# Attention on one Trainium2 core: blocks of probabilities kept whole and multiplied in fp32, or cut into two reduced-precision parts

## The chip, the cores and the metric

The kernel runs on one core of one Trainium2 chip. The metric is the time of one execution on the device in microseconds (us), as the median of several runs. An execution was also recorded by the hardware profiler, and all rows shown are from it. The engines are PE (TensorE matmul), PEld (its weight loads, which run beside the matmuls), DVE (VectorE), ACT (ScalarE), POOL (GpSimd) and SP (which issues most transfers).

## The reference

The program is two layers of a diffusion backbone over 1024 latent and 256 context tokens of width 1024, all in float32. The first layer mixes tokens by a chunked gMLP, the second by windowed attention; each is followed by a convolutional GLU. The change concerns the attention, in which 16 query heads share 4 key/value heads of 64 dimensions:

```
for each block of 128 queries j:
    kj, vj = k and v of blocks j-1, j, j+1
    s_lat  = (q @ kj^T) * 64^-0.5, masked to |q - k| <= 128
    s_ctx  = (q @ kc^T) * 64^-0.5                    # 256 context keys
    p      = softmax over [s_lat, s_ctx, sink]; the sink's column is dropped
    out[j] = p_lat @ vj + p_ctx @ vc
y = out @ w_o
```

So a query block sees five blocks of 128 keys: three of its window and two of the context. The first and the last query block have only two in the window, four in all.

## The kernel before

TensorE multiplies a full float32 operand in several passes. The kernel avoids that nearly everywhere: a float32 value is cut into two values of the type float32r, a high part (a cast, mostly on ACT) and a low part (value minus high part, on DVE), and a product of two such numbers is three single-pass matmuls (high by high, high by low, low by high).

In the attention the work is cut into 64 pairs of heads: 8 query blocks j, 4 key/value heads g, and two pairs `pr` for each. A loop over the pairs issues three steps, each for another pair, so that they overlap:

- `att_a` for pair i: the scores of two heads by TensorE (tiles `psA` and `psB` from `big`, the keys, and `tmp`, the queries), a masked running minimum of the negated scores on DVE (which leaves the scores in `tmp` for one head and in `wl` for the other, and the extremes in `sm`), the exponential on ACT, and the division on POOL.
- `att_b` for pair i - 2: each block of 128 keys of both heads is transposed by TensorE (`psB` from `ident` and `tmp` or `wl`), up to two blocks into one PSUM tile. The tile is then moved to SBUF in two parts: ACT casts it to the high part `PTh`, DVE subtracts that from the PSUM tile and writes the low part `PTl`. Both are tiles of the pool `act`, which has six buffers.
- `att_c` for pair i - 3: for each block the values `VV` (a tile called `y` in the profile, held as high part in 64 columns and low part in the other 64) are the weights, and `PTh` and `PTl` are multiplied one after the other, 256 columns each, into one PSUM tile `po`. The results by the high and the low part of the values stand in different partitions; ACT copies one half out (`tmp`) and DVE adds them into `row`.

Beside this the loop prepares queries (`q_prep`) and keys (`prep_k`, `build_k`), and, from pair 20 on, the output projection of finished rows of blocks (`o_steps`): attention rows go through DRAM (`oscr`) and come back as `oc`, to be multiplied with `wh` into `psA`. In pairs 8 to 23 the scores of the window and the context share one tile and one pass on DVE (`merged`).

The order on each engine is made by a scheduler from the order in which the loop issues the steps, its own estimates of durations, and the buffers. Each engine runs its instructions in that order and waits by semaphores. All instructions are issued through one helper, so all rows carry line 50, and it is the names of tiles that tell them apart.

Of the kernel before, what the change touches and what calls it, by code (L numbers as in the profile page):

```python
# [10 lines left out]
F32 = mybir.dt.float32  # L11
# [4 lines left out]
P = 128  # L16
# [16 lines left out]
def hybrid_kernel(  # L33
# [23 lines left out]
    V, S, G, T = Engine(nc.vector, "V"), Engine(nc.scalar, "S"), Engine(nc.gpsimd, "G"), Engine(nc.tensor, "T")  # L57
# [19 lines left out]
    def nm(s):  # L77
        uid[0] += 1
        return f"{s}_{uid[0]}"

    def t_raw():
        return sb.tile([P, 1024], F32, name=nm("raw"), tag="raw", bufs=3)
# [8 lines left out]
    def t_row(dt=F32, shape=(P, 1024)):  # L91
        return sb.tile(list(shape), dt, name=nm("row"), tag="row", bufs=10)
# [4 lines left out]
    def lead(tag):  # L97
        n = stage_pool["leads"].pop(tag, 0)
        if n:
            G.memset(stage_pool["pool"].tile([P, n], F32, name=nm("lead"), tag="lead" + tag, bufs=1), 0.0)  # L100

    def t_tmp(shape=(P, 640), dt=F32):
        return stage_pool["pool"].tile(list(shape), dt, name=nm("tmp"), tag="tmp", bufs=8)
# [5 lines left out]
    def t_act(shape=(P, 2, 640), dt=F32R):  # L109
        lead("act")  # L110
        return stage_pool["pool"].tile(list(shape), dt, name=nm("act"), tag="act", bufs=6)
# [21 lines left out]
    def psB(shape=(P, 512)):  # L133
        return ps.tile(list(shape), F32, name=nm("psB"), tag="psB", bufs=4)
# [1631 lines left out]
    qrows, qst, at = {}, {}, {}  # L1766
# [102 lines left out]
    def merged(j, g, pr):  # L1869
        return 8 <= 8 * j + 2 * g + pr < NM  # L1870
# [46 lines left out]
    run_post(20)  # L1917
    VV = hold["VV"]

    def att_b(j, g, pr):  # L1920
        nk = len(geo[j][1])
        Pt = at[(j, g, pr)]
        PTh, PTl = t_act((P, 5, 2, P)), t_act((P, 5, 2, P))
        for a in range(0, nk, 2):
            n = min(2, nk - a)
            pt = psB((P, 2, 2, P))
            for b in range(n):
                for h in range(2):
                    T.transpose(out=pt[:, b, h, :], in_=Pt[h][:, (a + b) * P:(a + b + 1) * P], identity=ident)
            S.copy(PTh[:, a:a + n], pt[:, 0:n])  # L1930
            V.tensor_sub(PTl[:, a:a + n], pt[:, 0:n], PTh[:, a:a + n])
        at[(j, g, pr)] = (PTh, PTl)

    orow, last_rows = {}, {}

    def att_c(j, g, pr):
        kts = geo[j][1]
        nk = len(kts)
        if merged(j, g, pr):
            kts = kts[-2:] + kts[:-2]  # L1940
        if j not in orow:
            orow[j] = t_row(shape=(P, KD, P))
        o = orow[j]
        PTh, PTl = at.pop((j, g, pr))
        po = psB((P, 2, P))
        for a in range(nk):
            lv = VV[:, kts[a], g, :]
            T.matmul(po, lv, PTh[:, a], start=(a == 0), stop=False)
            T.matmul(po, lv, PTl[:, a], start=False, stop=(a == nk - 1))
        ol = t_tmp((P, 2, P))  # L1950
        S.copy(ol[0:HD], po[HD:P])
        for h in range(2):
            V.tensor_tensor(out=o[h * HD:(h + 1) * HD, 2 * g + pr, :], in0=po[0:HD, h, :], in1=ol[0:HD, h, :],
                            op=ALU.add)
        if g == 3 and pr == 1:
            oh, ol_ = t_row(F32R, (P, KD, P)), t_row(F32R, (P, KD, P))
            S.copy(oh, o)
            V.tensor_sub(ol_, o, oh)
            if j >= 6:
                last_rows[j] = (oh, ol_)  # L1960
                return
            cs = slice(j * P, (j + 1) * P)
            S.dma_start(oscr[:, :, 0, cs], oh.bitcast(F32))
            Q.dma_start(oscr[:, :, 1, cs], ol_.bitcast(F32))
# [59 lines left out]
    for i in range(n_pairs + LC):  # L2024
        if i < n_pairs:
            j, g, pr = pairs[i]
            if j < 7 and pr == 1 and g in (1, 3):
                q_load(j + 1, g // 2)
            if pr == 1 and 1 < i < n_pairs - 1:
                q_prep(*pairs[i + 1][:2])  # L2030
            if i >= HEAD:
                att_a(j, g, pr)
            if j + 2 < 8:
                if g == 0 and pr == 1:
                    prep_k(j + 2)
                if g == 2 and pr == 0:
                    build_k(j + 2)
        if i in (21, 24, 27):
            t = 5 + (i - 21) // 3
            w = t_raw()[:, 0:512]  # L2040
            Q.dma_start(w, qraw[t - 5])
            qkv_post(t, 1, w)
        if i in (23, 26, 29):
            run_post()
        if LB <= i < n_pairs + LB:
            att_b(*pairs[i - LB])
        if LC <= i:
            att_c(*pairs[i - LC])
        while done < o_target(i):
            step(og)  # L2050
            done += 1
        tick()
# [68 lines left out]
```

## Time and profile before

| what | value |
|---|---|
| median of 3 runs | 2852.4 us (2848.68 to 2853.72) |
| the profiled execution | 2860.88 us, its span 2859.1 us |
| mean granted clock of TensorE | 0.988 of full |
| first score matmul of the loop to the last product with V | about 1797 to 2143 us |

The time of an execution is slightly longer than the span from the first to the last instruction. A busy share near 100% of PE does not say that TensorE is at its peak, because matmuls are pipelined and their rows overlap; the pace has to be read from the starts. Rows of groups give the busy time of all, the mean duration of one in ns, and the idle time before them with what ended it.

### The profile page before, as it was taken

The numbers are of one execution on the slowest core, as the hardware profiler recorded it, in microseconds if no ns is written. First come the engines' busy times: TensorE is split into PE (matmuls) and PEld (weight loads), VectorE is DVE, ScalarE is ACT, GpSimd is POOL, SyncE is SP. The second block draws the span as 40 slices with busy tenths as digits, with TensorE's granted clock in tenths as the row PEclk, the third lists the DMA queues.
The fourth block names the chain that finished last, engine by engine and source line by source line (L and its number), as shares of the span: only waits on it lengthen the run. The fifth ranks groups of instructions, "written<-read, shape, count | busy, mean of one in ns | idle before, by whom it ended". The sixth has DMA issues, their size and how long they took to land.

```text
span 2859.1 us, 40314 instructions
## 1 busy us (share of the span) xinstructions
PE 2741.8 (96%) x14570; PEld 2354.1 (82%) x14570; DVE 2221.8 (78%) x3466; ACT 1391.2 (49%) x2291; POOL 616.6 (22%) x806
## 2 busy tenths in 40 slices
PE   7999999999989999999999899999998999999998
PEld 5798887898889888888788778888887888888786
DVE  6567684787779899887776568898887788888776
ACT  4333242232367444455434545777876444445433
POOL 1164021360210212111000124543333121220000
PEclk9999999999999999999999999999999999999999
DMA  7775457554488355467855565347577345545753
GB/s 260 251 234 166 145 161 227 177 167 131 171 249 240 103 170 162 157 217 238 287 169 184 188 212 186 115 145 239 181 242 220 126 162 182 160 144 198 248 177 125
DMA packets 436335, 537.13 MB, mean 188 GB/s; under 512 B 20004, under 2 KB 300452, under 8 KB 436135
## 3 DMA queue, kind: packets, MB, share of 16 engines
q1 hardware_dynamic: 379575, 470.84, 51.4%
q10 hardware_dynamic: 55408, 59.52, 6.2%
q0 software_dynamic: 1152, 4.19, 0.4%
q8 instruction: 115, 1.88, 0.3%
q14 instruction: 85, 0.70, 0.1%
HBM read 414.40 MB, written 120.07 MB: 187 GB/s over the span
## 4 chain that ended last, share of the span: by engine, by line
PE 65%; DVE 13%; DMA 11%; ACT 5%; issue 4%; POOL 2%; SPq 1%; ACTq 0%; DVEq 0%; POOLq 0%
PE psB L50 48%; PE psA L50 16%; DVE row L50 3%; DVE wl L50 3%; DMA raw<-in_ada_w_dram 3%; DVE tmp L50 1%; DVE acc L50 1%; ACT wh L50 1%; ACT tmp L50 1%; DMA xT<-row 1%; DMA raw<-in_a_w_in_dram 1%; DVE y L50 1%; POOL sm L50 1%; DMA raw<-in_f_w_up_dram 1%; DMA raw<-in_f_w_down_dram 1%
## 5 line engine op out<-in xcount | busy, mean ns | idle before, releaser
L50 PE MATMUL psB<-cmb,wh 128*128 128x512 f32 (+2 forms) x2584 | 750.3, 374 | 7.2 <-ACT row L50 6.2
L50 PEld LDWEIGHTS psB<-cmb,wh 128*128 128x128 f32 x2584 | 471.9, 188 | 98.4 <-ACT row L50 8.1
L50 PE MATMUL psB<-cmb,wl 128*128 128x512 f32 (+2 forms) x1292 | 483.2, 374 | 0.2 <-DVE wl L50 0.2
L50 ACT CAST wh<-raw 128x1024 fp32r<-128x1024 f32 (+1 forms) x313 | 265.1, 863 | 441.6 <-PE psB L50 165.5
L50 DVE TENSOR_TENSOR wl<-raw,wh 128x1024 fp32r<-128x1024 f32 (+1 forms) x313 | 307.6, 997 | 106.6 <-ACT wh L50 104.9
L50 PEld LDWEIGHTS psB<-cmb,wl 128*128 128x128 f32 x1292 | 243.2, 188 | 44.0 <-DVE wl L50 0.8
L50 PE MATMUL psB<-wh,big 128*128 128x512 f32 x816 | 271.1, 398 | 3.7 <-ACT big L50 1.3
L50 ACT CAST wh<-row 128x1024 fp32r<-128x1024 f32 (+1 forms) x196 | 162.5, 834 | 186.8 <-DVE row L50 92.3
L50 PE MATMUL psB<-wh,act 128*128 128x512 f32 x640 | 200.1, 390 | 0.8 <-DVE tmp L50 0.8
L50 DVE TENSOR_TENSOR wl<-row,wh 128x1024 fp32r<-128x1024 f32 (+1 forms) x196 | 185.2, 948 | 12.2 <-ACT wh L50 11.8
L50 PE MATMUL psA<-big,wh 128*128 128x320 f32 x1024 | 193.2, 310 | 0.3 <-ACT row L50 0.3
L50 POOL TENSOR_TENSOR row<-raw,raw 128x512 f32<-128x512 f32 x44 | 68.5, 1558 | 574.2 <-DMA raw<-in_f_w_up_dram 490.8
L50 PEld LDWEIGHTS psB<-wh,big 128*128 128x128 f32 x816 | 154.3, 190 | 39.9 <-ACT tmp L50 2.4
L50 DVE SCALAR_TENSOR_TENSOR acc<-raw,ccols,acc 128x1024 f32<-128x1024 f32 x98 | 126.7, 1311 | 75.8 <-DMA raw<-in_ada_w_dram 75.5
L50 DVE SCALAR_TENSOR_TENSOR row<-row,cwcols,row 128x1024 f32<-128x1024 f32 (+2 forms) x142 | 152.6, 1075 | 39.2 <-ACT row L50 22.7
L50 ACT CAST ah<-raw 128x1024 fp32r<-128x1024 f32 x80 | 77.6, 974 | 201.6 <-PE psB L50 80.8
L50 DVE TENSOR_TENSOR row<-row,row 128x512 f32<-128x512 f32 (+4 forms) x169 | 155.9, 926 | 19.9 <-DMA row<-actd 12.2
L50 POOL TENSOR_SCALAR row<-row,sm,sm 128x128 f32<-128x128 f32 x160 | 144.1, 919 | 115.2 <-DMA row<-vscr 99.3
L50 PEld LDWEIGHTS psA<-big,wh 128*128 128x128 f32 x1024 | 159.9, 188 | 0.7 <-ACT row L50 0.5
L50 PE MATMUL psB<-wl,big 128*128 128x512 f32 x408 | 157.2, 395 | 0.9 <-DVE wl L50 0.9
L50 DVE TENSOR_TENSOR al<-raw,ah 128x1024 fp32r<-128x1024 f32 x80 | 90.2, 1128 | 71.9 <-ACT ah L50 71.6
L50 PE MATMUL psB<-row,wh 128*128 128x256 f32 x744 | 136.9, 286 | 8.2 <-ACT wh L50 6.7
(279 smaller groups left out, 6226.0 us busy)
## 6 DMA issues: line engine op xcount, KB each, us to landing
raw<-in_f_w_up_dram SPq DMA_DIRECT2D x121, 512.0 KB, 4.8
raw<-in_ada_w_dram SPq DMA_DIRECT2D x88, 512.0 KB, 4.4
raw<-in_a_w_in_dram SPq DMA_DIRECT2D x64, 512.0 KB, 4.8
wh<-woscr SPq DMA_DIRECT2D x48, 512.0 KB, 4.1
row<-actd SPq DMA_DIRECT2D x44, 512.0 KB, 5.5
actc<-row SPq DMA_DIRECT2D x44, 512.0 KB, 4.1
raw<-actc SPq DMA_DIRECT2D x40, 512.0 KB, 3.6
actd<-row SPq DMA_DIRECT2D x39, 512.0 KB, 2.7
```

Of the source, the lines that this page charges most:

```text
L50: ins = fn(*a, **kw)
```

## The change

In `att_b` some blocks stay whole: their transposed probabilities are copied once from PSUM to a float32 tile `PTw`, and no low part is made. For the first 20 pairs (the query blocks 0 and 1 and half of 2) these are blocks 0 to 3, later blocks 0, 1 and 4. The copy runs on ACT, except for blocks 2 and 3 of the first 20 pairs, where it runs on DVE. The remaining blocks are cut as before, and where there are at most two of them, high and low parts share one tile. In `att_c` a whole block is multiplied once, with the same values read as float32, in a full float32 product.

```diff
+    def whole(j, g, pr, a):
+        i = 8 * j + 2 * g + pr
+        return a < 4 if i < 20 else a in (0, 1, 4)
+
     def att_b(j, g, pr):
         nk = len(geo[j][1])
         Pt = at[(j, g, pr)]
-        PTh, PTl = t_act((P, 5, 2, P)), t_act((P, 5, 2, P))
+        wholes = [a for a in range(nk) if whole(j, g, pr, a)]
+        cut = [a for a in range(nk) if a not in wholes]
+        both = len(cut) > 2
+        PTw = t_act((P, 5, 2, P), F32) if wholes else None
+        PTh = t_act((P, 5, 2, P)) if cut else None
+        PTl = t_act((P, 5, 2, P)) if both else PTh
...
-            S.copy(PTh[:, a:a + n], pt[:, 0:n])
-            V.tensor_sub(PTl[:, a:a + n], pt[:, 0:n], PTh[:, a:a + n])
-        at[(j, g, pr)] = (PTh, PTl)
+            if a in wholes:
+                o = wholes.index(a)
+                (V.tensor_copy if a == 2 else S.copy)(PTw[:, o:o + n], pt[:, 0:n])
+                continue
+            o = cut.index(a)
+            ol = o if both else o + 2
+            S.copy(PTh[:, o:o + n], pt[:, 0:n])
+            V.tensor_sub(PTl[:, ol:ol + n], pt[:, 0:n], PTh[:, o:o + n])
+        at[(j, g, pr)] = parts
...
         for a in range(nk):
             lv = VV[:, kts[a], g, :]
-            T.matmul(po, lv, PTh[:, a], start=(a == 0), stop=False)
-            T.matmul(po, lv, PTl[:, a], start=False, stop=(a == nk - 1))
+            w = lv.bitcast(F32) if len(parts[a]) == 1 else lv
+            for n, x in enumerate(parts[a]):
+                T.matmul(po, w, x, start=(a == 0 and n == 0), stop=(a == nk - 1 and n == len(parts[a]) - 1))
```

The scheduler orders the stage anew. On PE, around the product with V of pair 28 (in the tile `psB_3056`; `act_3032` is its high part, `act_3033` its low part), there stands before:

```order
L50 MATMUL psB_3055_17986<-ident_69,tmp_3014_17789 128x128
L50 MATMUL psB_3055_17986<-ident_69,wl_3015_17790 128x128
L50 MATMUL psA_3007_17769<-wh_3039_17918,oc_3040_17920 128x512 x4
L50 MATMUL psB_3056_17991<-act_3032_17882,y_2391_14763 128x256
L50 MATMUL psB_3056_17991<-act_3033_17883,y_2391_14763 128x256
...
L50 MATMUL psA_3007_17769<-wh_3039_17918,oc_3040_17920 128x512 x2
L50 MATMUL psA_3064_18022<-big_2527_15607,tmp_3044_17943 128x384
```

High and low parts alternate, ten matmuls in all, with the projection's matmuls around them. On PE for the same pair (`act_3024` holds its three whole blocks, `act_3025` both parts of its two cut ones) there stands now:

```order
L50 MATMUL psB_3047_17815<-ident_69,tmp_3006_17629 128x128
L50 MATMUL psB_3047_17815<-ident_69,wl_3007_17630 128x128
L50 MATMUL psB_3048_17819<-act_3024_17717,y_2391_14763 128x256 x2
L50 MATMUL psB_3048_17819<-act_3025_17718,y_2391_14763 128x256 x4
L50 MATMUL psB_3048_17819<-act_3024_17717,y_2391_14763 128x256
L50 MATMUL psA_2999_17609<-wh_3031_17748,oc_3032_17750 128x512 x6
L50 MATMUL psA_3056_17847<-big_2527_15607,tmp_3036_17773 128x384
```

Seven instructions stand for ten, of which three are full float32 products, and the projection's six matmuls follow in one piece. On DVE, at `att_b` of pair 12 (low part `act_2760`; `ISA` is the masked minimum, with its extremes in `sm`), there stands before:

```order
L50 ISA wl_2756_16607,sm_2752_16603<-psA_2758_16616,mask_14494,nsnk_14504 128x640
L50 ISA sm_2752_16603 128x1
L50 TENSOR_TENSOR act_2760_16633<-psB_2761_16634,act_2759_16632 128x512
L50 TENSOR_TENSOR act_2760_16633<-psB_2762_16641,act_2759_16632 128x512
L50 TENSOR_TENSOR act_2760_16633<-psB_2763_16648,act_2759_16632 128x256
L50 ISA tmp_2772_16680,sm_2769_16677<-psA_2774_16682,mask_14494,nsnk_14504 128x640
```

On DVE for the same pair (whole blocks `act_2751`, the cut one `act_2752`) there stands now:

```order
L50 ISA wl_2748_16531,sm_2744_16527<-psA_2750_16540,mask_14494,nsnk_14504 128x640
L50 ISA sm_2744_16527 128x1
L50 COPY act_2751_16556<-psB_2754_16564 128x512
L50 TENSOR_TENSOR act_2752_16557<-psB_2755_16570,act_2752_16557 128x256
L50 TENSOR_TENSOR row_2710_16377<-psB_2756_16575,tmp_2757_16582 64x128 x2
L50 ISA tmp_2764_16598,sm_2761_16595<-psA_2766_16600,mask_14494,nsnk_14504 128x640
```

Two wide subtractions gave way to one copy between the same minima, and the final addition of an earlier pair moved up.

More of the change, by code (lines that the diff above doesn't have):

```diff
@@ L1922, in att_b @@
         Pt = at[(j, g, pr)]
-        PTh, PTl = t_act((P, 5, 2, P)), t_act((P, 5, 2, P))
+        wholes = [a for a in range(nk) if whole(j, g, pr, a)]
[4 more added lines that the diff above has]
+        PTl = t_act((P, 5, 2, P)) if both else PTh
+        parts = {}
+        for a in range(nk):
+            n = cut.index(a) if a in cut else wholes.index(a)
+            parts[a] = (PTw[:, n],) if a in wholes else (PTh[:, n], PTl[:, n if both else n + 2])
         for a in range(0, nk, 2):
@@ L1943, in att_c @@
         o = orow[j]
-        PTh, PTl = at.pop((j, g, pr))
+        parts = at.pop((j, g, pr))
         po = psB((P, 2, P))
```

## Prediction

> **What bounds the kernel now.** I read the totals of the page first, then the attention stage in windows, then who ends the waits of PE there, then its chain of waits, and last the timeline for the pace of single matmuls. All durations are of the profiled execution.
>
> ```profile
> span 2859.1 us, 40314 instructions
> PE 2741.8 (96%) x14570; PEld 2354.1 (82%) x14570; DVE 2221.8 (78%) x3466; ACT 1391.2 (49%) x2291; POOL 616.6 (22%) x806
> ```
>
> PE is the engine of this kernel. The change lies in the attention stage alone, from the first scores (1797 us) to the last product with V (2143 us). The windows row gives for a stretch: length, then busy time and instructions of PE, PEld, DVE, ACT and POOL, the granted clock, the DMA share and GB/s.
>
> ```profile
> 1797.00:1937.00 140.00, 130.17 (x959) 118.11 (x958) 126.27 (x372) 112.34 (x274) 72.17 (x119) 0.99 0.42 136
> 1937.00:2143.00 206.00, 195.05 (x1337) 175.07 (x1335) 175.00 (x601) 155.54 (x356) 66.81 (x96) 0.98 0.66 218
> 1797.00:2143.00 346.00, 325.22 (x2293) 293.18 (x2291) 301.27 (x973) 267.88 (x629) 138.98 (x214) 0.99 0.56 185
> ```
>
> I cut at 1937 because pair 25 is multiplied with V there. Up to it DVE is busy 90% and PE 93%; behind it PE is at 95% and DVE at 85%. The chain of waits of the two stretches says the same in another way:
>
> ```profile
> by line: PE psB L50 27.9%; PE psA L50 16.6%; DVE tmp L50 8.7%; DVE act L50 7.4%; issue 7.2%; ACT act L50 5.2%; ACT tmp L50 4.9%; DVE row L50 4.9%; DMA qraw<-act 4.7%; ACT wl L50 4.1%; DVE wl L50 4.1%; ACT big L50 1.0%; DVE raw L50 0.9%; DVE
> ...
> by line: PE psB L50 40.7%; PE psA L50 32.4%; DMA oscr<-row 4.7%; DMA oc<-oscr 4.5%; ACT tmp L50 2.5%; issue 2.5%; DVE row L50 2.2%; ACT act L50 2.1%; DMA raw<-in_b_w_o_dram 1.8%; DVE tmp L50 1.4%; ACT wl L50 1.3%; DVE wl L50 0.9%; ACT acc L
> ```
>
> In the first stretch PE holds 44% of the chain, and the other engines' evictions and softmax rows most of the rest; in the second PE holds 73%. What PE waits for in the whole stage (us, times, longest):
>
> ```profile
> PE psB L50 <- DVE sm L50: 5.7, 7, 1.6
> PE psB L50 <- DVE act L50: 4.6, 8, 1.4
> PE psA L50 <- DMA oc<-oscr: 3.9, 2, 2.4
> PE psA L50 <- DVE sm L50: 2.9, 5, 1.0
> PE psB L50 <- ACT tmp L50: 1.5, 4, 0.9
> PE psB L50 <- DVE row L50: 0.6, 2, 0.3
> ```
>
> PE's idle time is 346 - 325.2 = 20.8 us, of which these rows name 19.2: DVE ends 13.8, ACT 1.5, the transfer of rows for the output projection 3.9. The true room is a little larger, because a matmul's row goes on after the next one could start: a product with V has a row of 0.28 us at a pace of 0.12 (below), so each of some 28 waits hides another 0.16 us, 4 us in all. So PE has about 25 us of room: 12.5 before 1937, 12.5 behind it.
>
> **What an fp32 product costs PE.** In the built program one fp32 product is one instruction, but the trace shows how the chip runs it: the two products of `ones` with a whole fp32 tile near 114 us have four matmul rows and four weight loads.
>
> ```profile
> 113.86 1.88 PE L50 MATMUL psA<-row,ones 128*128 128x512 f32 x4
> ...
> 114.30 0.19 PEld L50 LDWEIGHTS psA<-row,ones 128*128 128x128 f32 x1 [0.24 <-issue]
> 114.73 0.19 PEld L50 LDWEIGHTS psA<-row,ones 128*128 128x128 f32 x1 [0.24 <-issue]
> 115.16 0.19 PEld L50 LDWEIGHTS psB<-wh,big 128*128 128x128 f32 x1 [0.24 <-issue]
> ```
>
> The loads stand 0.43 us apart, so a record with 512 columns holds PE for 0.43 us, and a product, two records, for 0.86. A block of probabilities has 256 columns (two heads of 128): half of that, 0.43 us for the two records. Today a block takes two single-pass products, high and low part:
>
> ```profile
> 1962.03 1.40 PE L50 MATMUL psB<-act,y 128*128 128x256 f32 x10
> 1963.27 0.62 PE L50 MATMUL psA<-wh,oc 128*128 128x512 f32 x2
> ...
> 1962.01 1.23 PEld L50 LDWEIGHTS psB<-act,y 128*128 128x128 f32 x10 [0.25 <-DVE sm L50]
> 1963.16 0.30 PEld L50 LDWEIGHTS psA<-wh,oc 128*128 128x128 f32 x2
> ```
>
> Ten of them take 1.24 us by the matmul rows (1962.03 to 1963.27) and 1.15 by the weight loads: 0.25 or 0.23 us for a block. So a whole block costs PE 0.18 to 0.20 us more. I take 0.19, since the two rows lie that close.
>
> **The sum.** Whole blocks: pairs 0 to 19 four each, 80; pairs 20 to 55 three each, 108; pairs 56 to 63 have four blocks, of which two are whole, 16. Together 204. PE gains 204 x 0.19 = 39 us of work: 95 blocks up to pair 24, 18 us; 109 behind, 21 us.
>
> What DVE and ACT are spared goes by these rows:
>
> ```profile
> L50 DVE TENSOR_TENSOR act<-psB,act 128x512 fp32r<-128x512 f32 x128 | 83.3, 683 | 8.4 <-ACT act L50 8.2
> L50 DVE TENSOR_TENSOR act<-psB,act 128x256 fp32r<-128x256 f32 x48 | 19.9, 414 | 0.3
> L50 ACT CAST act<-psB 128x512 fp32r<-128x512 f32 x128 | 70.1, 588 | 28.9 <-PE psB L50 24.9 <-DMA qraw<-act 2.5 <-DMA oscr<-row 0.4
> L50 DVE COPY row<-psA 128x1024 f32<-128x1024 f32 x1 | 1.2, 1215 | 0.0
> ```
>
> 84 of the 128 wide subtractions go (57 us) and 36 of the 48 narrow ones (15 us). In pairs 0 to 19 DVE takes over one wide copy each; the trace has no wide copy from a PSUM bank, half of the 1.2 us copy of two banks is 0.61, and the subtraction's 0.68 is the other bound; I take 0.61: 12 us. DVE is spared 60 us, 21 before 1937 and 39 behind. ACT is spared the 20 casts that DVE takes over, 12 us; its other copies to fp32 I take at the cast's price, 0.588, bounded by nothing better than that row and costing nothing either way, since ACT is idle 78 us in the stage.
>
> None of the 60 us counts as such. DVE stands between PE's scores and transposes, and what it gives back is at most the waits of PE that it ends: 13.8 us, with ACT's 1.5 and the hidden ends about 19. Nor does all of that come back: the softmax behind a score runs through DVE, ACT and POOL one after the other, and at the ends of rows of tiles a long DVE step remains. I take two thirds in the first stretch, 8 of 12.5 us, and half in the second, 6 of 12.5, where 3.9 us wait for a transfer that the change doesn't touch. So: 18 - 8 = +10 us up to pair 24, 21 - 6 = +15 behind, together +25. The lower end is all 25 us of room filled at the lower price: 204 x 0.18 - 25 = +12; the upper end is nothing recovered at the higher, 204 x 0.20 = +41.
>
> Small things. The product with V of a whole block waits for one eviction instead of a cast and a subtraction, so it is ready earlier; its cover, the next pair's transposes and scores, stays. A pair of the first row takes one `act` buffer instead of two, others two as before: no new wait. DMAs are as many as before. The order of PE changes: the projection's matmuls (`wh,oc`) stand behind a pair's product in one piece of six instead of four before it and two behind. If their rows of `oscr` are late, PE has less to do meanwhile; the two waits of 3.9 us could double, and if transposes cover them they vanish, so -4 to +4, and I take 0. Behind 2143 the output projection and the second feed-forward layer start later by what the stage grew.
>
> The profiled execution took 2860.88 us, 8.5 above the median of the runs shown, 2852.4. The difference of +25 is made in the former and added to the latter: I predict **2877 us**, +0.9%. About 0.2% (5.7 us) is what a measurement of this kernel can tell from no change.
>
> **The rivals.**
> *PE has more room than its busy time says.* Weight loads are busy 293 of 346 us, and the change leaves their number as it is: two for a block, before and after. If the weight path, not the stream of columns, set PE's pace, 53 us of room would take the 39 us, and the time would stay at 2852. For it: 10 loads in 1.15 us today, hardly a gap. Against it: near 114 us the loads stand idle 0.24 us between each other while the columns stream. The Trainium skill, Perfetto Trace Analysis, section "Identifying the Most-Contended Engine", has this as a rule: matmul busy time is a poor measure of PE's headroom, and the share of weight-load time a better one. By that rule the answer is this rival's; the spaced loads of the fp32 products speak for the columns. Chance 0.08.
>
> *DVE was the bound all along, and the time follows it.* Place: pairs 0 to 24. With 21 us off DVE there and 39 behind, all waits that DVE and ACT end would go, and PE would hide the rest: about -15 us, 2837. That needs a whole block to cost no more than today's plus the room over the blocks, 0.25 + 25/204 = 0.37 us; the rows say 0.43, and a single pass (0.12) would contradict the four records. Chance 0.05.
>
> *Nothing comes back.* PE waits for the softmax's latency, not for DVE's load; then the full price stands: +37 to +41, 2889 to 2893. For it: in the second stretch DVE is idle 31 us and PE waits for `sm` all the same. Chance 0.14.
>
> *The longer products with V delay the rows' way through DRAM.* At two ends of rows PE waits 4 us or more for `oscr` and `oc`; with products and projection in larger pieces these grow, and the sum passes 2896. Chance 0.05.
>
> The forecast (+12 to +34) keeps 0.68. With the full price it makes 0.82, which is the range 2857 to 2896: below +12 stand the 4 us of transfer waits that may vanish and 4 us of granted clock (0.98 of full over 206 us) that a fuller PE may win back, +4 in all; above +41 some 3 us of longer transfer waits. Slower 0.68 + 0.14 + 0.05 = 0.87, same 0.08, faster 0.05.
>
> **What would show it.** In the changed kernel's trace the products with V should be 608 matmul rows and 608 weight loads as before, since two records replace two; a burst with four whole blocks should take 4 x 0.43 us and more. Matmuls should start 0.21 us apart there. DVE's busy time in the stage should fall by about 60 us and PE's rise; PE's waits for `sm` and `act` should shrink to less than half, and both stretches should be longer. The prediction is wrong if the fp32 records follow each other in 0.12 us, if the first stretch gets shorter by more than its 8 us of recovered waits can hold, or if time moves outside the attention stage.

## The result, and the profile after

The changed kernel takes 2884.4 us (median of 5 runs, 2876.4 to 2885.7) where the kernel before takes 2852.4 in runs on the same chip: the ratio is 1.0108 (95% interval 1.0097 to 1.0119), some 31 us slower. The profiled execution took 2884.75 us. Its totals:

```profile
span 2883.0 us, 40226 instructions
PE 2771.7 (96%) x14570; PEld 2381.1 (83%) x14570; DVE 2175.0 (75%) x3366; ACT 1382.7 (48%) x2271; POOL 619.8 (21%) x806
```

PE has as many matmuls and loads as before, 14570, and is busy 30 us longer; DVE is busy 47 us less. The windows rows (length, then busy time of PE, PEld, DVE, ACT and POOL, granted clock, DMA) cut the execution ahead of the attention stage, at it and behind it; I take the stage from the first score matmul to the start of the last product with V. After:

```profile
0.00:1791.90 1791.90, 1728.96 (x8887) 1483.31 (x8888) 1352.23 (x1790) 789.47 (x1151) 372.28 (x468) 0.99 0.61 194
1791.90:2165.80 373.90, 358.83 (x2301) 321.51 (x2301) 259.21 (x876) 260.81 (x614) 139.96 (x214) 1.00 0.54 173
2165.80:2883.00 717.20, 683.91 (x3387) 576.31 (x3385) 563.55 (x701) 332.46 (x508) 107.56 (x124) 0.98 0.53 173
```

The same cuts in the profile of the kernel before:

```profile
0.00:1796.70 1796.70, 1731.11 (x8886) 1483.92 (x8887) 1353.12 (x1790) 788.74 (x1151) 370.01 (x468) 0.99 0.61 194
1796.70:2144.70 348.00, 326.77 (x2301) 294.51 (x2301) 303.06 (x976) 269.83 (x633) 138.98 (x214) 0.99 0.56 185
2144.70:2859.10 714.40, 683.93 (x3386) 575.67 (x3384) 565.59 (x701) 332.63 (x509) 107.58 (x124) 0.98 0.53 174
```

The stage grew from 348.0 to 373.9 us, by 25.9. Ahead of it, where the change reaches nothing, this execution of the kernel before was 4.8 us later; behind it the changed one is 2.8 longer. In sum that is 23.9, while the medians differ by 32.

The clock column accounts for most of the difference. In some stretches of a few us the granted clock falls to half, in other places in each execution. In the stage of the kernel before:

```profile
1811.70:1816.70 5.00, 3.59 (x19) 3.54 (x19) 3.15 (x11) 2.45 (x7) 2.45 (x5) 0.69 0.78 283
1976.70:1981.70 5.00, 1.31 (x11) 0.87 (x9) 4.99 (x16) 4.49 (x13) 1.60 (x5) 0.91 0.52 168
1981.70:1986.70 5.00, 5.00 (x19) 4.62 (x20) 0.51 (x2) 0.74 (x2) 1.47 (x2) 0.50 0.94 348
1986.70:1991.70 5.00, 5.00 (x28) 4.26 (x28) 4.52 (x9) 2.10 (x6) 0.00 (x0) 0.90 0.64 191
```

Length times missing clock, (1 - clock) x 5 us, adds up to 1.7 us in the first stretch and 3.4 in the second; in the changed kernel's stage to nothing. If PE is on the path there, the stage of the kernel before without these losses is 348.0 - 5.1 = 342.9 us, and the growth is 31 us. A second profile of the kernel before (experiment 11) supports the subtraction: 346.4 us with 3.4 lost, so 343.0. Below, a length "without clock losses" is made in this way. A shift of some 1.5 us in one stretch counts for nothing, since the two profiles of the kernel before differ by as much there (138.3 and 139.8 in the first, 204.6 and 203.3 in the second). Lengths of stretches go by starts to 0.01 us; the windows shown are cut to 0.1.

What PE waits for in the changed kernel's stage (us, times, longest), up to the product of pair 25:

```profile
PE psB L50 <- ACT act L50: 1.6, 1, 1.6
PE psB L50 <- ACT tmp L50: 1.4, 2, 0.8
PE psA L50 <- DVE sm L50: 1.2, 2, 0.9
PE psB L50 <- DVE wl L50: 0.7, 1, 0.7
PE psB L50 <- DVE sm L50: 0.4, 1, 0.4
```

and behind it:

```profile
PE psB L50 <- ACT act L50: 4.5, 3, 1.6
PE psA L50 <- DMA oc<-oscr: 2.5, 2, 1.5
PE psA L50 <- DVE sm L50: 1.3, 2, 0.7
```

Of the 13.8 us of waits that DVE ended before, 3.6 are left: 1.2, 0.7, 0.4 and 1.3. But a new one stands in their place: 6.1 us for `act`, ended by ACT, which now makes most of the whole blocks alone. Behind pair 25 the three rows sum to 8.3 us.

The price of a product is seen in the starts of bursts. A burst is the product with V of one pair, and a record is one row of a matmul in the trace, of which an fp32 product has two. The burst of pair 29 (three whole blocks and two cut, ten records) and what PE starts next:

```profile
1962.84 2.03 PE L50 MATMUL psB<-act,y 128*128 128x256 f32 x10
1964.52 1.76 PE L50 MATMUL psA<-wh,oc 128*128 128x512 f32 x6
```

From start to start 1.68 us, where ten single-pass records took 1.24. In the trace the records of whole blocks start 0.215 us apart, those of cut blocks 0.115. Over the stage the product with V stands in one row, 608 matmuls as before; the two other rows are the copies of whole blocks and their like on DVE:

```profile
L50 PE MATMUL psB<-act,y 128*128 128x256 f32 x608 | 125.3, 369 | 7.0 <-ACT act L50 4.6 <-ACT tmp L50 0.8 <-DVE wl L50 0.7
L50 DVE COPY act<-psB 128x512 f32<-128x512 f32 x20 | 13.7, 685 | 0.2 <-PE psB L50 0.2
L50 DVE TENSOR_TENSOR act<-psB,act 128x512 fp32r<-128x512 f32 x44 | 30.2, 687 | 6.3 <-ACT act L50 6.0
```

The same row before:

```profile
L50 PE MATMUL psB<-act,y 128*128 128x256 f32 x607 | 87.2, 290 | 5.2 <-DVE sm L50 4.0 <-DVE act L50 0.4 <-DVE row L50 0.3
```

125.3 - 87.2 = 38.1 us more, over 204 whole blocks 0.187 us each.

### The profile page after: what moved, and what is told of

The parts are those of the page before. It is cut to its first block, busy times and chain, and to the rows that moved or that the text cites. A ratio compares the mean times of both kernels' runs of the same rounds, so it can differ in the third digit from the quotient of the medians.

```text
span 2883.0 us, 40226 instructions
## 1 busy us (share of the span) xinstructions
PE 2771.7 (96%) x14570; PEld 2381.1 (83%) x14570; DVE 2175.0 (75%) x3366; ACT 1382.7 (48%) x2271; POOL 619.8 (21%) x806
## 4 chain that ended last, share of the span: by engine, by line
PE 67%; DVE 11%; DMA 10%; issue 4%; ACT 4%; POOL 2%; SPq 1%; ACTq 0%; DVEq 0%; POOLq 0%
PE psB L50 50%; PE psA L50 17%; DVE row L50 3%; DMA raw<-in_ada_w_dram 3%; DVE wl L50 3%; ACT wh L50 1%; DVE acc L50 1%; DVE tmp L50 1%; SPq L50 1%; DMA raw<-in_f_w_up_dram 1%; DVE y L50 1%; DMA xT<-row 1%; ACT tmp L50 1%; POOL sm L50 1%; ACT row L50 1%
```

## The experiments

Stage lengths are up to the product of pair 25 and behind it, as profiled, with the clock loss in brackets; "stage" is their sum without losses, set against 342.9 before. Every ratio is to the kernel before on the same chip.

| kernel | ratio to before | first stretch | second stretch | stage, against before |
|---|---|---|---|---|
| before | 1 | 140.0 (1.7) | 208.0 (3.4) | 342.9 |
| after | 1.0108 [1.0097, 1.0119] | 149.5 (0) | 224.5 (0) | 373.9, +31 |
| 1 price alone | 1.0135 [1.0116, 1.0153] | 159.8 (3.5) | 226.0 (3.4) | 378.9, +36 |
| 2 relief alone | 1.0004 [0.9992, 1.0016] | 135.4 (0) | 206.0 (1.7) | 339.7, -3 |
| 3 first 20 pairs alone | 1.0026 [1.0017, 1.0036] | 145.5 (0) | 206.8 (3.4) | 348.9, +6 |
| 4 later pairs alone | 1.0076 [1.0055, 1.0098] | 143.8 (0) | 222.1 (0) | 365.9, +23 |
| 5 single pass | 0.9922 [0.9907, 0.9937] | 127.6 (0) | 193.8 (0) | 321.5, -21 |
| 6 all whole | 1.0156 [1.0141, 1.0172] | 152.2 (0) | 238.5 (1.7) | 389.0, +46 |
| 7 fifth block on DVE | 1.0088 [1.0073, 1.0103] | 148.2 (0) | 222.6 (0) | 370.8, +28 |
| 8 two blocks, first 25 pairs | 1.0059 [1.0037, 1.008] | 157.3 (5.1) | 207.8 (3.4) | 356.6, +14 |
| 9 as 8, with `tmp` | 1.0046 [1.0029, 1.0063] | 149.0 (1.7) | 206.1 (3.4) | 350.0, +7 |
| 10 single pass, fifth block on DVE | 0.991 [0.9896, 0.9925] | 126.3 (0) | 192.6 (1.7) | 317.2, -26 |

The scheduler orders every kernel anew, so each experiment changes, beside its edit, the order of work on the engines. Even in experiment 1, which has the casts and subtractions of the kernel before, only some 880 of DVE's 980 rows of the stage stand in the same order as before, by the names of their tiles. No run holds the order still, so a difference of a few us between two experiments may be the order's.

### 1. The price alone

The casts and subtractions of the kernel before stay, and only the products of the 204 blocks become fp32, on the high part; the low part is left out of the product.

```diff
+            if a < 4 if 8 * j + 2 * g + pr < 20 else a in (0, 1, 4):
+                T.matmul(po, lv.bitcast(F32), PTh[:, a].bitcast(F32), start=(a == 0), stop=(a == nk - 1))
+                continue
```

> All blocks are cut as before the change (same casts and subtractions), but the 204 blocks that the change keeps whole are multiplied in full float32 from their high part alone (the low part is made and left out of the product). If the price of the float32 products on PE makes the change's time (about 0.16 us a block by the bursts after it), this kernel is as slow as the changed one or slower, +32 to +39 us over before, about 2887. If the changed one lost its time to new waits for its whole copies or to its new order, this kernel, which keeps the old evictions, is at most 10 us slower than before, about 2860.

Measured 2892.3 us, +38 by the ratio, as the first branch forecast. Windows, the two stretches:

```profile
1791.80:1951.60 159.80, 148.58 (x957) 132.43 (x957) 127.02 (x371) 112.08 (x275) 71.57 (x118) 0.98 0.40 129
1951.60:2177.60 226.00, 217.91 (x1347) 192.78 (x1346) 179.31 (x607) 158.52 (x361) 67.04 (x96) 0.98 0.60 197
```

Both stretches are 18.0 us longer without clock losses (156.3 against 138.3, 222.6 against 204.6). DVE does the work of the kernel before (busy 127.0 and 179.3 us, 126.1 and 176.9 before), so this is the price about as the stage pays it: 36 us, 0.18 per block. The changed kernel's stage grew by 31, so all the relief is worth some 5 us.

### 2. The relief alone

As the changed kernel, but a whole block is rounded to float32r as it is copied and multiplied twice in a single pass, so that PE has the work of before; the low part is left out.

```diff
-        PTw = t_act((P, 5, 2, P), F32) if wholes else None
+        PTw = t_act((P, 5, 2, P)) if wholes else None
-            parts[a] = (PTw[:, n],) if a in wholes else ...
+            parts[a] = (PTw[:, n], PTw[:, n]) if a in wholes else ...
-            w = lv.bitcast(F32) if len(parts[a]) == 1 else lv
+            w = lv
```

> Whole blocks are copied once, on the same engines as in the change, but as float32r, and each is multiplied twice in a single pass from that copy (in place of high and low part): PE's work is that of before, DVE is spared 60 us and ACT 12 us. If DVE's load stood behind part of PE's waits, the time falls by 5 to 15 us, to about 2842. If PE waited for the latency of the softmax and not for DVE's load, nothing changes, 2852. If the new evictions or the new order cost the time, it rises by 10 us or more, to 2862 and above.

Measured 2855.0 us, no change. Windows:

```profile
1795.00:1930.40 135.40, 126.06 (x950) 115.30 (x950) 108.84 (x334) 102.11 (x252) 71.17 (x118) 1.00 0.42 135
1930.40:2136.40 206.00, 198.53 (x1354) 178.23 (x1354) 149.67 (x544) 158.54 (x363) 71.03 (x96) 0.99 0.69 225
```

DVE is spared 17 us of 126 in the first stretch and 27 of 177 in the second; the stage is 3 us shorter, all of it in the first. What PE waits for shows what took DVE's place, in the stage and just behind it (the row of `acc` stands behind it):

```profile
PE psB L50 <- ACT act L50: 9.6, 13, 1.7
PE psB L50 <- POOL acc L50: 3.9, 1, 3.9
PE psA L50 <- DVE sm L50: 1.8, 4, 0.6
PE psB L50 <- DVE act L50: 0.7, 2, 0.4
PE psB L50 <- DVE sm L50: 0.6, 2, 0.4
```

DVE's waits are nearly gone, and ACT's copies into `act` hold PE 9.6 us instead, 6.2 of them behind pair 25. In that stretch PE's waits sum to 7.1 us where they were 11.1, and it is no shorter: a matmul's row goes on after the next could start (0.28 us at a pace of 0.12) and hides the beginning of a wait. The weight loads' rows, which are shorter, show the exchange more fully: there DVE ended 10.5 us of their waits for `sm` before, and here ACT ends 11.9 for `act`. That DVE was the bound all along falls with this run: it would have given 15 us and gives nothing in the total.

### 3 and 4. The two sets of pairs apart

```diff
-        return a < 4 if i < 20 else a in (0, 1, 4)
+        return a < 4 if i < 20 else False          # 3: 80 blocks
+        return False if i < 20 else a in (0, 1, 4) # 4: 124 blocks
```

> Only the first 20 pairs keep four blocks whole (80 blocks), later pairs cut all. By price less recovered waits: 80 x 0.16 = 13 us less 5 to 8, so +5 to +9 us, about 2859. If DVE bounds these pairs: not slower than before, 2845 to 2852.

> Only the pairs from 20 on keep blocks whole (124 blocks), the first 20 cut all. By price less recovered waits: 124 x 0.16 to 0.19 = 20 to 24 us less about 4, so +16 to +20, about 2871, and with the early kernel's gain or loss it adds up to the changed kernel's +32. If the two parts hinder each other only together (buffers, order), the two sum to less than +20.

Measured 2861.2 us (+7 by the ratio) and 2876.1 (+22): together 29 of the whole's 31, so the two sets hardly act on each other. The first is within its forecast, the second a little above it. A whole block costs 0.09 us in the first 20 pairs and 0.17 in the later ones: there the relief buys next to nothing.

### 5. One single pass

As experiment 2, with each copy multiplied once. PE has 204 records less than before; the low part is left out.

```diff
-        PTw = t_act((P, 5, 2, P), F32) if wholes else None
+        PTw = t_act((P, 5, 2, P)) if wholes else None
-            w = lv.bitcast(F32) if len(parts[a]) == 1 else lv
+            w = lv
```

> As the kernel that only relieves DVE and ACT, but each whole block (a float32r copy) is multiplied once in a single pass; its low part is left out. PE has 204 single-pass products of 0.117 us less than before, 24 us. If PE's work sets the stage's length, the time falls by 15 to 24 us, to about 2833. If latency of the softmax and waits for evictions set it, PE only waits longer and the time falls by less than 8 us, to 2845 or above.

Measured 2829.8 us, 22 below before and 25 below experiment 2. Windows:

```profile
1792.20:1919.80 127.60, 117.13 (x857) 104.77 (x857) 109.62 (x337) 101.66 (x255) 71.62 (x118) 1.00 0.45 144
1919.80:2113.70 193.90, 185.82 (x1244) 163.52 (x1243) 147.18 (x539) 156.45 (x360) 71.73 (x96) 1.00 0.71 237
```

A record takes 0.115 us, so 204 of them are 23.5 us. Against experiment 2, whose copies are the same, the ratios differ by 23 us and the stages by 18 (339.7 to 321.5): the time follows PE's passes in this direction too, in the stage for some three quarters.

### 6. All blocks whole

```diff
-        return a < 4 if i < 20 else a in (0, 1, 4)
+        return True
```

> All 304 blocks stay whole, none is cut: 100 float32 products more than the changed kernel, 100 x 0.165 = 16 us for PE, and some 35 us less for DVE. If DVE's time is worth nothing any more, +48 us over before, about 2900; if DVE's relief still pays, +32 to +40, 2885 to 2892.

Measured 2898.3 us, 14 above the changed kernel for 100 more whole blocks, 0.14 us each. That is near the forecast for relief that is worth nothing any more (2900): more relief does not turn the balance.

### 7. The fifth block's copy on DVE

```diff
-                (V.tensor_copy if a == 2 else S.copy)(PTw[:, o:o + n], pt[:, 0:n])
+                (V.tensor_copy if a in (2, 4) else S.copy)(PTw[:, o:o + n], pt[:, 0:n])
```

> The changed kernel with the fifth block's whole copy (36 pairs from pair 20 on) moved from ACT to DVE, which it left with time to spare. If PE's new waits for ACT's copies (6 us by its matmul rows, up to 13 by its weight loads) lengthen the stage, the time falls by 4 to 10 us against the changed kernel, to about 2877. If these waits only take the place of others, it stays at 2884.

Measured 2876.0 us, 8 below the changed kernel's median (6 by the ratios); its stage is 3 us shorter, and the rest lies behind it (714 us against 717) and ahead. PE's waits on ACT for `act` in the stage and just behind it fall from 6.1 to 4.3 us:

```profile
PE psB L50 <- POOL acc L50: 4.6, 1, 4.6
PE psB L50 <- ACT act L50: 4.3, 3, 1.5
```

The total is what the expectation gave for ACT's copies as a limit, but the stage's 3 us say that it was a small one. With the same 204 blocks in fp32, this kernel is still 25 us slower than before.

### 8 and 9. Two whole blocks, and the `act` buffers

Experiment 8 keeps two blocks whole, in the first 25 pairs alone, where DVE is busiest. Experiment 9 holds the whole blocks in the pool `tmp` where three blocks are cut.

```diff
-        return a < 4 if i < 20 else a in (0, 1, 4)
+        return a < 2 if i < 25 else False
```

```diff
-        PTw = t_act((P, 5, 2, P), F32) if wholes else None
+        PTw = (t_tmp((P, 2, 2, P)) if both else t_act((P, 5, 2, P), F32)) if wholes else None
```

> Only two blocks (the first PSUM tile) stay whole, and only in pairs 0 to 24, where DVE is busiest: 50 blocks, 50 x 0.165 = 8 us for PE; DVE is spared 25 subtractions, 17 us. By price less recovered waits (at most the 5 us by which the kernel with relief alone was shorter there) +3 us, about 2855, no gain. If DVE bounds these pairs, it is the best of all, 2845 to 2849.

> The kernel with two early whole blocks took a third tile of the pool act for each of the pairs 8 to 24 (whole, high, low; the pool has six), and was 17 us longer up to pair 25 than before, where price alone gives 8. Here the whole copy of these pairs lies in the pool tmp instead, and act gives two tiles a pair as before. If the third tile made the loss, the kernel comes to the +3 us expected of price less recovered waits, 2853 to 2858. If not, it stays near 2870.

Both came out slower than expected: 2871.7 us (+17 by the ratio) and 2864.5 (+13). In 8, three blocks are cut, so `both` is true, and a pair takes three tiles of the six in `act` instead of two. The first stretch of 8, and then of 9:

```profile
1793.90:1951.20 157.30, 142.40 (x960) 127.43 (x960) 114.35 (x344) 113.08 (x274) 72.12 (x118) 0.97 0.40 126
```

```profile
1794.20:1943.30 149.10, 139.74 (x960) 125.54 (x960) 113.44 (x344) 112.70 (x274) 71.25 (x118) 0.99 0.40 132
```

8 us lie between them, 5 without clock losses: that much is put down to the third tile, though the order differs as well. The remaining +9 in 9 (147.3 against 138.3) are the price of its 50 blocks at 0.18. Nothing came back, with DVE spared 13 us of 126. In its waits, too, ACT has taken DVE's place:

```profile
PE psB L50 <- ACT tmp L50: 2.9, 3, 1.8
PE psB L50 <- ACT act L50: 2.7, 2, 2.1
PE psA L50 <- DVE sm L50: 1.4, 2, 0.8
```

By the ratios both are further from before than by the stage; their runs had a mean granted clock of 0.988 to 0.991 (8: at most 0.989) where most of before's had 0.991, and 0.002 of the whole execution is some 6 us.

### 10. Experiments 5 and 7 together

Each whole block is multiplied once in a single pass (the low part is left out), and the fifth block's copy runs on DVE.

> The kernel with a single pass for each whole block (low part left out), and the fifth block's copy of pairs 20 to 55 on DVE instead of ACT. If the waits for ACT's copies lengthen the stage here as in the changed kernel (8 us there), it takes 2822 to 2826; if another wait takes their place, 2830.

Measured 2825.7 us, the fastest kernel of the study, but with fewer digits than the kernel before computes. It is 4 us below experiment 5, and its stage too: so the first branch holds, and moving the fifth copy off ACT pays a little here as well. It also says what the passes cost: the changed kernel with its fp32 products and the same copies (experiment 7) takes 50 us longer. By the records 204 products of 0.43 us in place of 0.115 are 64 us, so some 10 us are not paid; PE's waits in the stage are 17.0 us here and 11.5 there.

### 11. The kernel before, profiled again

> The kernel before once more, for a second profile: its attention stage should be 348 us long within 2 us, and begin 3 to 5 us earlier than in the first profile, where all kernels tried since begin it.

One execution: 2855.9 us, span 2854.1, stage 346.4 us, as expected; it begins 2.5 us earlier than in the first profile, not 3 to 5:

```profile
1794.20:2140.60 346.40, 325.29 (x2301) 293.05 (x2301) 303.03 (x976) 269.63 (x633) 138.51 (x214) 0.99 0.56 186
```

## Why the prediction was right, and where it was not

The prediction was 2877 us (2857 to 2896), slower; it came out 7 higher. The mechanism was right: PE pays the passes, and DVE's relief gives back a small part. How near the number came is in part luck, as two errors of the second stretch, price and relief, have opposite signs.

**What bounds.** PE, as the prediction read it: experiments 1, 2 and 5 move PE's passes and DVE's work apart, and the time follows the passes.

**The price.** 204 x 0.19 = 39 us. The product's rows give 38.1, the records stand 0.215 us apart, half of the 0.43 that was read off the products with `ones`, and the stage pays 36 (experiment 1). Of the split, the first stretch's 18 is what was measured; the second paid 18 instead of 21, 3 less, and PE's waits there are 4 us shorter. That longer bursts hid them is the reading that fits. PE's waits behind pair 25, in the kernel before and then in experiment 1:

```profile
PE psB L50 <- DVE sm L50: 4.8, 5, 1.6
PE psA L50 <- DMA oc<-oscr: 3.9, 2, 2.4
PE psB L50 <- DVE act L50: 2.2, 4, 0.8
PE psB L50 <- ACT tmp L50: 0.2, 1, 0.2
```

```profile
PE psB L50 <- DVE sm L50: 3.4, 4, 1.5
PE psA L50 <- DMA oc<-oscr: 1.9, 1, 1.9
PE psB L50 <- DVE act L50: 1.4, 2, 1.2
PE psB L50 <- ACT act L50: 0.4, 1, 0.4
PE psB L50 <- ACT tmp L50: 0.2, 1, 0.2
```

They sum to 11.1 and 7.3 us, the changed kernel's (above) to 8.3: what the relief took from DVE's rows there, ACT's row for `act` took back.

**The relief.** This is the mis-sized term. The prediction took 8 us back in the first stretch and 6 in the second. Experiment 1 against the changed kernel, without clock losses: the first stretch gets 6.8 back (156.3 to 149.5), the second nothing (222.6 to 224.5). So up to pair 25 the stage grew 11 us where 10 stood in the sum, and behind it 20 where 15 stood. The step that failed is "half in the second, 6 of 12.5": it took every wait that DVE ended as one that a freer DVE could give back, and did not ask who is late next. The next is ACT, whose copy a product now waits for directly: in the second stretch ACT ends 4.5 us of waits for `act` and DVE 1.3, where DVE ended 7.0 before. The prediction costed ACT at nothing, "since ACT is idle 78 us in the stage"; it is idle still, and late all the same. The changed kernel's trace shows how. ACT takes its instructions in the scheduler's order, and a copy stands behind whatever is ahead of it. So it is at the second of the three waits for ACT behind pair 25:

```profile
2086.29 1.07 ACT L50 ACTIVATE tmp<-acc 128x1024 bf16<-128x1024 f32 x1
...
2087.34 1.05 ACT L50 ACTIVATE tmp<-acc 128x1024 bf16<-128x1024 f32 x1
...
2088.38 0.58 ACT L50 COPY act<-psB 128x512 f32<-128x512 f32 x1
...
2089.01 1.25 PE L50 MATMUL psB<-act,y 128*128 128x256 f32 x5 [1.56 <-ACT act L50]
```

The transposes for this copy had ended by about 2086.8, but ACT was still at two passes over `acc`, in which the output projection ends, of 1.07 and 1.05 us. The same two passes stand ahead of the copy at 1988.3 (a wait of 1.4 us), a 1.0 us cast of weights (`wh`) at 2163.7 (1.5), and in the first stretch a cast that waits for DVE at 1912.3 (1.6). At the first two places PE waited 1.3 and 1.5 us before as well, put down to DVE's `sm`, and in experiment 2 1.5 and 1.6 us, put down to ACT. Experiment 2 shows that the exchange happens without any fp32 product, and experiments 7 and 10 that moving copies off ACT gives back a few us. A kernel that keeps all copies on ACT and only moves these passes behind them was not run.

**DVE's 60 us.** By mean durations, 84 x 0.683 + 36 x 0.414 - 20 x 0.685 = 59 us are gone. The durations of DVE's rows in the stage sum to 56 us less (362 to 306), but its busy time fell by 44 (303.1 to 259.2), because busy time counts rows that run into each other once. Of the two bounds for a copy from one PSUM bank, 0.61 and 0.68, the upper was right. Neither matters to the time.

**The profile against the median.** The sum was made against an execution 8.5 us above its median and then added to the median. That hid a part of the answer: the excess is as large as the clock it lost, 5.1 us in the stage itself and some 3.5 us ahead of it (15.4 us lost there against 11.9 in the changed kernel). So the 23.9 us between the two profiled executions lie near the predicted 25 by luck alone. The changed kernel's stage lost none in its profiled execution. The prediction had "4 us of granted clock" that could come back as a bound only. Whether the change makes the losses rarer is open: the two profiles of before and that of experiment 1 lost 3.4 to 6.9 us in the stage, after and experiments 4, 5 and 7 none, the other experiments 1.7 to 8.5, but that is one execution of each.

**Behind the stage.** Taken as a mere shift, it grew by 2.8 us, 0.8 of it lost clock. Time that moves outside the stage was one of the prediction's signs of being wrong; over all kernels profiled, this part takes 713.2 to 717.2 us. PE's first transposes of `acc` there wait 3.7 us for POOL, 0.5 before. But experiment 1 has that wait too, 4.3 us, and its time behind the stage is as before, 714.2. So the cause of the rest stays open.

**The rivals.** Room for the weight loads falls: their number stayed, and the time still grew by the whole price in experiment 1. The loads' busy time even rose with the slower products, from 294.5 to 321.5 us in the stage, although the count is the same. By the rule of the Trainium skill (Perfetto Trace Analysis, "Identifying the Most-Contended Engine"), which judges PE's headroom not by matmul busy time but by MFU (the work done over the peak) and the share of weight-load time, the loads left 53 us free; no run here agrees. DVE as the bound falls with experiment 2. "Nothing comes back" is right for the second stretch and for experiment 9, wrong for the first 20 pairs. There the change also takes 20 casts off ACT, which experiment 9 does not; that fits, but no run separates the two reliefs. Longer waits for `oscr` did not come: 2.5 us for `oc` instead of 3.9.

**What was to show it.** 608 matmuls, records 0.21 us apart, both stretches longer: so. A burst with four whole blocks, "4 x 0.43 us and more":

```profile
1852.78 2.13 PE L50 MATMUL psB<-act,y 128*128 128x256 f32 x10
1854.75 1.49 PE L50 MATMUL psA<-big,tmp 128*128 128x256 f32 x12
```

1.97 us from start to start. The waits for `sm` and `act` did not fall to less than half: 13.2 us before (5.7, 4.6 and 2.9), 9.0 after (6.1, 2.5 and 0.4). DVE's part of them did, from 13.2 to 2.9.

## What to carry to other kernels

In this stage, where PE is busy 93 to 95%, extra passes per operand were paid nearly in full, and of the 44 us that the change took off DVE's busy time some 5 came back: read the passes from the starts of records, not from the number of instructions. A wait that an engine ends is not a stock of time that relieving this engine gives back; before counting it, ask which engine ends it next, and what stands ahead of that engine's step in its own order: an engine that is idle for a quarter of the stage can still be late where it counts. And add a predicted difference to the median only after looking at what the profiled execution lost that others did not, the clock first.

## What the runs showed of the hardware

An fp32 product shows as two records of twice the length of a single-pass one: 0.215 us against 0.115 at 256 columns, so that a product costs 0.43 us where high and low part cost 0.23. On DVE a plain fp32 copy from a PSUM tile of 128x512 takes as long as the subtraction that reads the PSUM tile and another operand, 685 and 687 ns; a copy of 128x256 takes 416 ns from PSUM (36 in experiment 7) and 328 from SBUF (two in the kernel before). The Trainium skill (VectorE: DVE Perf Modes, "Why PSUM operands drop a tier") says that a PSUM operand holds fp32 work at the basic rate; the slower copy from PSUM agrees. In this stage the clock came down to half for 3.4 or 6.8 us at a time, at other places in each execution, and cost one execution of the kernel before 5.1 us in this stage and another 3.4.
